# Adaptive modulation weights as 64 rows by two column halves: two transposes per chunk in place of four

## The chip, the cores and the metric

The kernel runs on one core of a Trainium2 chip. Its engines are TensorE (PE, with its weight loads shown as PEld), VectorE (DVE), ScalarE (ACT), GpSimd (POOL) and SyncE (SP), which issues most of the loads and stores. Each engine works through its own queue in order and waits on semaphores for the others. The metric is the device time of one execution in microseconds, the median of several runs. Lower is better.

## The reference

Two decoder layers over 1024 tokens of width 1024, all in float32: first an mLSTM layer, then a layer of multi-head latent attention, each followed by a squared-ReLU MLP. Every norm is modulated by vectors that are computed from one condition vector `c`:

```python
def modulate(h, shift, scale):
    return h * (1 + scale[:, None, :]) + shift[:, None, :]

cond = jax.nn.silu(c)                              # (1, 1024)
for l in range(2):
    ada = cond @ ada_w[l] + ada_b[l]               # (1, 6144) from a 1024 x 6144 matrix
    sh1, sc1, g1, sh2, sc2, g2 = jnp.split(ada, 6, axis=-1)
    h = modulate(rmsnorm(x, norm_g[l, 0]), sh1, sc1)
    ...                                            # mixer: mLSTM (l = 0) or latent attention (l = 1)
    x = x + g1[:, None, :] * rmsnorm(y, norm_g[l, 1])
    h = modulate(rmsnorm(x, norm_g[l, 2]), sh2, sc2)
    y = jnp.square(jax.nn.relu(h @ mlp_w1[l])) @ mlp_w2[l]
    x = x + g2[:, None, :] * rmsnorm(y, norm_g[l, 3])
# before the attention layer, for the shared keys and values:
kv_shift, kv_scale = jnp.split(cond @ kv_ada_w + kv_ada_b, 2, axis=-1)
```

The change touches only `cond @ ada_w + ada_b` and `cond @ kv_ada_w + kv_ada_b`: vector times matrix, one number per column.

## The kernel before

Activations are kept with features on the 128 partitions and 512 tokens (one of two halves of the sequence) along the free dimension. Every large product is done as three matmuls on a high and a low part of each operand (`mm3`, lines 299 to 301). Weights are loaded by SP into one of four buffers `raw` of 128 x 1024 (`fill_raw`, line 266); `wsplit` makes the high part on ScalarE (line 246) and the low part on VectorE (line 247), into a ring of eight buffers `ws`. `split_mod` does the same for activations (lines 520 and 521). Line 255 is a helper under which evacuations and other prompt steps are recorded, line 259 the copy out of PSUM.

The modulation vectors are not computed on TensorE, apart from the first two, but on VectorE beside the other work. A chunk is 512 columns of the matrix, with its 1024 rows as eight blocks of 128. `ada_chunk` loads the chunk in four quarters, each of two row blocks. A quarter goes into a `raw` buffer as one load of 512 KB; while `spare[0]` is set, into an `hd` buffer (a ring of eight, line 403); and while `apart[0]` is set, into two of six `tmc` buffers, as two loads of 256 KB (line 398). Row blocks lie on the partitions, so block `k` is multiplied by `cond[:, k:k+1]`, one number per partition, and added to the accumulator `acc`, the only buffer `tma` (lines 409 and 411): eight VectorE instructions of 512 columns. After two further turns of the generator `ada_turn` transposes the four blocks of 128 columns of `acc` on TensorE into a PSUM buffer `pc` (line 383), VectorE sums over the 512 columns in groups of 128 (line 385), which gives four numbers per partition, and adds the bias (line 386). So each column of the matrix ends on one partition, in the form in which the norms use it.

There are 24 chunks: eight for layer 0 (`bg0`), four for keys and values and four for layer 1 (`bg1`), and eight more for layer 1 (`bg_rest`). They are generators, advanced one step at a time beside the dense work: `with_bg` and the loop over `og0` in the first layer; `behind(bg_latent(), 5)` beside the first MLP, with `apart[0]`; `bg_rest` as the filling of `two_streams` beside the rest of that MLP and the attention of the first half.

The order on TensorE around these places is fixed by `issue_after` edges (`go`, `in_turn`), and the sums are put behind an instruction of the dense stream by `paced`. What else runs on VectorE, ScalarE and SP is put in order, when the program is built, by the framework's own model of how long instructions take, with a priority for `wload` and `evac`. That model also chooses which `raw` buffer a load takes.

Other lines that the prediction names: 889 scales the output of an mLSTM chunk on VectorE, and 915 transposes it on TensorE; 1151 loads stored sums (`s`) for the MLP into `raw`, 1290 and 1291 load weights of the MLP's second matrix; 1666 is another sum over rows, of 128 columns, in the same accumulator `tma`; 1918 is the sum over a row of attention scores, and 2027 transposes the attention's probabilities through `pc`.

Of the kernel before, what the change touches and what calls it, by code (L numbers as in the profile page):

```python
# [9 lines left out]
F32 = mybir.dt.float32  # L10
# [4 lines left out]
ALU = mybir.AluOpType  # L15
AX = mybir.AxisListType

P = 128
# [3 lines left out]
KD = D // P  # L22
# [60 lines left out]
def kernel(  # L83
# [27 lines left out]
    nc = tc.nc  # L111
# [4 lines left out]
    ts = lambda i, n: slice(i * n, (i + 1) * n)  # L116
# [21 lines left out]
    def tmc(dt=F32):  # L138
        return sb.tile([P, 512], dt, tag="tmc", bufs=TMC, name=f"tmc_{next(uid)}")

    def tma():
        return sb.tile([P, 512], F32, tag="tma", bufs=1, name=f"tma_{next(uid)}")

    def small(n, dt=F32):
        return sb.tile([P, n], dt, tag=f"sm{n}", bufs=6, name=f"sm_{next(uid)}")

    def ps():
        return pp.tile([P, 512], F32, tag="ps", bufs=2, name=f"ps_{next(uid)}")

    def pc():  # L150
        return pp.tile([P, 512], F32, tag="pc", bufs=2, name=f"pc_{next(uid)}")
# [7 lines left out]
    def const(shape, dt, name):  # L159
        return sb.tile(shape, dt, tag=name, bufs=1, name=name)  # L160
# [70 lines left out]
    def paced():  # L231

        return tc.issue_after(pace[0]) if pace[0] else nullcontext()
# [59 lines left out]
    def wcols(w, c0, n=P, k0=0, nk=KD):  # L293
        return w[k0 * P : (k0 + nk) * P, c0 : c0 + n].rearrange("(k p) n -> p k n", p=P)
# [37 lines left out]
    cond = const([P, KD], F32, "cond")  # L332
# [44 lines left out]
    ada = const([P, 2, 48], F32, "ada")  # L377
    kvada = const([P, 16], F32, "kvada")

    def ada_turn(acc, bias, dst):  # L380
        pt = pc()
        for j in range(4):
            nc.tensor.transpose(pt[:, ts(j, P)], acc[:, ts(j, P)], ident)
        s = small(4)
        nc.vector.reduce_sum(s, pt.rearrange("p (j k) -> p j k", k=P), axis=AX.X)
        nc.vector.tensor_add(dst, s, bias)
        yield

    late, apart, spare = [False], [False], [False]

    def ada_chunk(w, c0, bias, dst):

        acc = tma()
        for q in range(4):
            if apart[0]:
                r = [tmc(), tmc()]
                for kk in range(2):
                    nc.sync.dma_start(r[kk], w[ts(2 * q + kk, P), c0 : c0 + 512])
            else:
                r = (hdv if spare[0] else raw)()  # L400
                if not spare[0]:
                    r = r.rearrange("p (a b) -> p a b", b=512)
                nc.sync.dma_start(r, wcols(w, c0, 512, 2 * q, 2))
                r = [r[:, 0], r[:, 1]]
            for kk in range(2):
                k = 2 * q + kk
                with paced():
                    if k == 0:
                        nc.vector.tensor_scalar(acc, r[kk], cond[:, 0:1], None, ALU.mult)
                    else:  # L410
                        nc.vector.scalar_tensor_tensor(
                            acc, r[kk], cond[:, k : k + 1], acc, ALU.mult, ALU.add
                        )
            yield
        yield
        late[0] = True
        yield "wait"
        late[0] = False
        yield from ada_turn(acc, bias, dst)

    def ada_part(l, part):
        for j in (2 * part, 2 * part + 1):
            yield from ada_chunk(
                ada_w[l], j * 512, col(AB + l * 48 + j * 4, 4), ada[:, l, ts(j, 4)]
            )

    def ada_kv(part):
        for j in (2 * part, 2 * part + 1):
            yield from ada_chunk(kv_ada_w, j * 512, col(KVB + j * 4, 4), kvada[:, ts(j, 4)])
# [2180 lines left out]
    acc = [m0[:, 0], m0[:, 1], m1[:, 0], m1[:, 1], ps(), ps()]  # L2610
# [64 lines left out]
    def chain(*gs):  # L2675
        for g in gs:
            yield from g() if callable(g) else g
# [65 lines left out]
        drain(wide)  # L2743

    bgs = chain(bg0, bg1)
    with tc.issue_after(loaded):
        for b in range(4):
            nc.sync.dma_start(
                xt_d[0][2 * b * P : (2 * b + 2) * P].rearrange("(k p) n -> p k n", p=P), xT0.t[b]
            )  # L2750
# [375 lines left out]
```

## Time and profile before

| | |
|---|---|
| time, median of 3 runs | 2269.22 us (2268.82 to 2272.16) |
| the profiled execution: time, span | 2272.61 us, 2270.8 us |
| granted TensorE clock, mean | 0.997 of full |
| TensorE busy | 2238.3 us, 99% |
| VectorE busy | 1669.0 us, 73% |
| ScalarE busy | 1113.0 us, 49% |
| moved by DMA | 494.60 MB, mean 218 GB/s |

The span goes from the first to the last instruction of the profiled execution; its time has a little around it. Busy times are unions of an engine's instructions; matmuls are pipelined and overlap in the rows, so the sum of single durations is more than the busy time. In a row of the profile, `L411 DVE SCALAR_TENSOR_TENSOR tma<-raw,cond,tma x103: 732/746/754` means line 411, on VectorE, output and inputs by the program's names without buffer numbers, 103 instructions, and shortest, median and longest duration in ns. `SPq` is SP's queue, where issuing a load is an instruction of its own.

### The profile page before, as it was taken

How to read it: one execution, taken by the hardware profiler on the slowest of the kernel's cores; microseconds unless marked ns; L12 is line 12 of the kernel's file. 1: busy time of each engine (PE TensorE's matmuls, PEld its weight loads, DVE VectorE, ACT ScalarE, POOL GpSimd, SP SyncE). 2: the span in 40 equal slices, each digit the busy share in tenths (PEclk: the TensorE clock that was granted, in tenths of full speed). 3: DMA queues.
4: the chain of work that ended last, by engine and by line, in shares of the span. 5: the costliest groups of instructions: out<-in, count | busy, mean ns of one | idle time of the engine just before them, and what ended most of it. 6: DMA issues, size and time to landing. Idle time of an engine off the chain costs nothing.

```text
span 2270.8 us, 30938 instructions
## 1 busy us (share of the span) xinstructions
PE 2238.3 (99%) x11050; PEld 1852.5 (82%) x11050; DVE 1669.0 (73%) x2717; ACT 1113.0 (49%) x1937; POOL 137.8 (6%) x238
## 2 busy tenths in 40 slices
PE   8999999999999999999999999999999999999998
PEld 6888888888887887778888877888888888888887
DVE  6677777889887787677774787777758967675556
ACT  4455434765434445544455555545545433464343
POOL 1000000001122220000000000000010111100000
PEclk9999999999999999999999999999999999999999
DMA  9544455667999888567687764874487777665431
GB/s 313 186 135 123 148 166 150 194 213 267 323 282 310 280 285 297 178 216 221 208 269 224 262 226 146 285 281 177 156 259 275 240 248 222 234 220 187 149 101 57
DMA packets 404651, 494.60 MB, mean 218 GB/s; under 512 B 29236, under 2 KB 270961, under 8 KB 404497
## 3 DMA queue, kind: packets, MB, share of 16 engines
q1 hardware_dynamic: 384320, 421.74, 57.7%
q0 software_dynamic: 20176, 70.89, 8.6%
q8 instruction: 87, 1.43, 0.3%
q14 instruction: 68, 0.55, 0.1%
HBM read 366.19 MB, written 126.35 MB: 217 GB/s over the span
## 4 chain that ended last, share of the span: by engine, by line
PE 82%; DVE 6%; DMA 5%; issue 4%; ACT 3%; POOL 0%; SPq 0%; DVEq 0%; ACTq 0%; POOLq 0%
PE ps L299 13%; PE ps L300 13%; PE ps L301 13%; PE pm L300 9%; PE pm L301 9%; PE pm L299 9%; DMA raw<-in_mlp_w_dram 2%; PE pc L299 2%; PE pc L301 2%; PE pc L300 2%; DVE wl L247 1%; PE pc L2113 1%; DMA raw<-s 1%; DVE k L255 1%; DMA lw<-wh 1%
## 5 line engine op out<-in xcount | busy, mean ns | idle before, releaser
L246 ACT CAST wh<-raw 128x1024 fp32r<-128x1024 f32 (+4 forms) x295 | 298.6, 1014 | 399.0 <-PE ps L300 140.4
L247 DVE TENSOR_TENSOR wl<-raw,wh 128x1024 fp32r<-128x1024 f32 (+4 forms) x295 | 347.8, 1181 | 173.9 <-ACT wh L246 147.0
L299 PE MATMUL ps<-k,wh 128*128 128x512 f32 x1109 | 438.9, 396 | 2.7 <-DVE k L521 1.2
L301 PE MATMUL ps<-k,wl 128*128 128x512 f32 x1109 | 432.6, 390 | 0.0
L300 PE MATMUL ps<-k,wh 128*128 128x512 f32 x1109 | 432.1, 390 | 0.0
L299 PEld LDWEIGHTS ps<-k,wh 128*128 128x128 f32 x1109 | 208.3, 188 | 50.1 <-issue 3.2
L301 PEld LDWEIGHTS ps<-k,wl 128*128 128x128 f32 x1109 | 208.2, 188 | 44.1
L300 PEld LDWEIGHTS ps<-k,wh 128*128 128x128 f32 x1109 | 208.4, 188 | 42.9 <-issue 1.4
L299 PE MATMUL pm<-wh,hd 128*128 128x512 f32 x488 | 191.6, 393 | 0.0
L301 PE MATMUL pm<-wh,hd 128*128 128x512 f32 x488 | 190.0, 389 | 0.0
L300 PE MATMUL pm<-wl,hd 128*128 128x512 f32 x488 | 189.9, 389 | 0.0
L255 DVE TENSOR_TENSOR k<-k,pm 128x512 f32<-128x512 f32 (+1 forms) x170 | 141.1, 858 | 63.7 <-PE pm L301 63.6
L300 PEld LDWEIGHTS pm<-wl,hd 128*128 128x128 f32 x488 | 91.7, 188 | 19.3 <-issue 0.5
L301 PEld LDWEIGHTS pm<-wh,hd 128*128 128x128 f32 x488 | 91.6, 188 | 19.1
L299 PEld LDWEIGHTS pm<-wh,hd 128*128 128x128 f32 x488 | 91.6, 188 | 19.1 <-issue 0.5
L299 PE MATMUL pm<-hd,wk 128*128 128x512 f32 x256 | 101.5, 396 | 2.0 <-ACT hd L520 2.0
L300 PE MATMUL pm<-hd,wk 128*128 128x512 f32 x256 | 100.2, 391 | 0.4 <-DVE hd L521 0.4
L301 PE MATMUL pm<-hd,wk 128*128 128x512 f32 x256 | 100.0, 391 | 0.0
L300 PE MATMUL pm<-hd,wh 128*128 128x512 f32 x256 | 99.6, 390 | 0.2 <-DVE hd L521 0.2
L299 PE MATMUL pm<-hd,wh 128*128 128x512 f32 x256 | 99.3, 390 | 0.5 <-ACT hd L520 0.5
L301 PE MATMUL pm<-hd,wl 128*128 128x512 f32 x256 | 99.6, 389 | 0.0
L1007 ACT ACTIVATE tmp<-tmp 128x512 f32<-128x512 f32 x80 | 50.4, 630 | 80.1 <-DVE tmp L255 71.0
(510 smaller groups left out, 4750.7 us busy)
## 6 DMA issues: line engine op xcount, KB each, us to landing
raw<-in_mlp_w_dram SPq DMA_DIRECT2D x158, 512.0 KB, 4.9
raw<-in_mlp_w_dram SPq DMA_DIRECT2D x128, 256.0 KB, 4.7
raw<-in_ada_w_dram SPq DMA_DIRECT2D x54, 512.0 KB, 4.7
raw<-in_a_w_in_dram SPq DMA_DIRECT2D x44, 512.0 KB, 4.0
lo<-wl POOLq DMA_DIRECT2D x32, 512.0 KB, 6.1
u<-k POOLq DMA_DIRECT2D x32, 512.0 KB, 5.2
raw<-s SPq DMA_DIRECT2D x32, 512.0 KB, 4.3
wk<-lo SPq DMA_DIRECT2D x64, 256.0 KB, 4.4
```

What stands on the lines that cost most here:

```text
L246: nc.scalar.copy(hi[:, :n], r[:, :n])
L247: i = nc.vector.tensor_sub(lo[:, :n], r[:, :n], hi[:, :n].bitcast(F32))
L255: return f(*a, **k)
L299: nc.tensor.matmul(o, lh, rh, start=start, stop=False)
L300: nc.tensor.matmul(o, lh, rl, start=False, stop=False)
L301: pe_last[0] = nc.tensor.matmul(o, ll, rh, start=False, stop=stop)
L1007: nc.scalar.activation(s, s, AF.Relu)
L2113: nc.tensor.transpose(pt[:, ts(m, P)], u.prs[i][kb // 4][:, ts(kb % 4, P)], ident)
```

## The change

A chunk keeps its 512 columns and 1024 rows but lies otherwise on the partitions: partitions 0 to 63 hold the first 256 columns and partitions 64 to 127 the second 256 columns, of the same 64 rows. So a chunk is 16 row blocks of 64 rows, of 256 columns each. A quarter has four of these blocks and is loaded in two parts, one for each half of the partitions (two buffers `tmc` in four). The multipliers have to lie accordingly: `cond2[64 g + p, 2 k + e]` is `cond[64 e + p, k]` for both halves `g`, made by four small copies. The accumulator has 256 columns, so there are two blocks to transpose; after the transposition the two halves lie beside each other along the free dimension, and the sum goes over groups of 64. The four numbers come in the order (block, half), and the addition of the bias puts them into the order of the columns.

```diff
+    cond2 = const([P, 2 * KD], F32, "cond2")
+
+    def halves_of_cond():
+        v = cond2.rearrange("p (k e) -> p k e", e=2)
+        for g in range(2):
+            for e in range(2):
+                nc.vector.tensor_copy(v[ts(g, 64), :, e], cond[ts(e, 64)])
+
     def ada_turn(acc, bias, dst):
-        pt = pc()
-        for j in range(4):
+        pt = pc()[:, :256]
+        for j in range(2):
             nc.tensor.transpose(pt[:, ts(j, P)], acc[:, ts(j, P)], ident)
         s = small(4)
-        nc.vector.reduce_sum(s, pt.rearrange("p (j k) -> p j k", k=P), axis=AX.X)
-        nc.vector.tensor_add(dst, s, bias)
+        nc.vector.reduce_sum(s, pt.rearrange("p (a k) -> p a k", k=64), axis=AX.X)
+        v = lambda t: t.rearrange("p (g j) -> p j g", j=2)
+        nc.vector.tensor_add(v(dst), s.rearrange("p (j g) -> p j g", g=2), v(bias))
         yield
...
-        acc = tma()
+        acc = tma()[:, :256]
+        by = lambda r: r.rearrange("p (a b) -> p a b", b=256)
         for q in range(4):
             if apart[0]:
-                r = [tmc(), tmc()]
-                for kk in range(2):
-                    nc.sync.dma_start(r[kk], w[ts(2 * q + kk, P), c0 : c0 + 512])
+                r = [by(tmc()), by(tmc())]
             else:
-                r = (hdv if spare[0] else raw)()
-                if not spare[0]:
-                    r = r.rearrange("p (a b) -> p a b", b=512)
-                nc.sync.dma_start(r, wcols(w, c0, 512, 2 * q, 2))
-                r = [r[:, 0], r[:, 1]]
-            for kk in range(2):
-                k = 2 * q + kk
+                r = [by((hd if spare[0] else raw)())]
+            n = 4 // len(r)
+            for i, t in enumerate(r):
+                for g in range(2):
+                    rows, c = 256 * q + 64 * n * i, c0 + 256 * g
+                    nc.sync.dma_start(
+                        t[ts(g, 64)],
+                        w[rows : rows + 64 * n, c : c + 256].rearrange("(k r) n -> r k n", r=64),
+                    )
+            for i in range(4):
+                a, k = r[i // n][:, i % n], 4 * q + i
                 with paced():
                     if k == 0:
-                        nc.vector.tensor_scalar(acc, r[kk], cond[:, 0:1], None, ALU.mult)
+                        nc.vector.tensor_scalar(acc, a, cond2[:, 0:1], None, ALU.mult)
                     else:
                         nc.vector.scalar_tensor_tensor(
-                            acc, r[kk], cond[:, k : k + 1], acc, ALU.mult, ALU.add
+                            acc, a, cond2[:, k : k + 1], acc, ALU.mult, ALU.add
                         )
             yield
...
     bgs = chain(bg0, bg1)
+    halves_of_cond()
```

## The prediction

> **What bounds the kernel now.** I read the page from the top, then the tile that the change touches, then the places where the chain of waits leaves TensorE. First the page's span, its busy times and its chain's shares:
>
> ```profile
> span 2270.8 us, 30938 instructions
> ...
> PE 2238.3 (99%) x11050; PEld 1852.5 (82%) x11050; DVE 1669.0 (73%) x2717; ACT 1113.0 (49%) x1937; POOL 137.8 (6%) x238
> ...
> PE 82%; DVE 6%; DMA 5%; issue 4%; ACT 3%; POOL 0%; SPq 0%; DVEq 0%; ACTq 0%; POOLq 0%
> ```
>
> TensorE is busy for all but 32 us, so TensorE work that disappears is worth its own time, unless something else is then late. The other engines cost time only where the chain passes through them. Next the tile view of `tma`, the accumulator of the modulation sums:
>
> ```profile
> L411 DVE SCALAR_TENSOR_TENSOR tma<-raw,cond,tma x103: 732/746/754, 57.3 to 1243.1; 128x512 f32<-128x512 f32 x103
> ...
> L383 PE MATMUL pc<-ident,tma x96: 270/272/330, 93.8 to 1244.9; 128*128 128x128 f32 x96
> ...
> L1666 DVE SCALAR_TENSOR_TENSOR tma<-tmc,ada,tma x21: 343/352/353, 759.1 to 819.7; 128x128 f32<-128x128 f32 x21
> ...
> L409 DVE TENSOR_SCALAR tma<-raw,cond x15: 475/479/488, 56.8 to 1190.2; 128x512 f32<-128x512 f32 x15
> ...
>   DMA raw<-in_kv_ada_w_dram: 11.2, 4
> ```
>
> The 96 transposes at four a chunk say that there are 24 chunks, between 57 and 1245 us. The last row says that VectorE stood still four times, 11.2 us together, for weights of such a chunk.
>
> **Transposes: 48 go.** A transpose shows as 272 ns, but neighbours overlap; what counts is how far four of them push the next matmul. One of the 24 places, in order of time:
>
> ```profile
> 581.37 0.39 PE L300 MATMUL ps<-k,wh 128*128 128x512 f32 x1
> 581.59 0.39 PE L301 MATMUL ps<-k,wl 128*128 128x512 f32 x1
> 581.82 0.60 PE L383 MATMUL pc<-ident,tma 128*128 128x128 f32 x4
> 582.18 0.47 PE L299 MATMUL ps<-k,wh 128*128 128x512 f32 x1
> 582.49 0.39 PE L300 MATMUL ps<-k,wh 128*128 128x512 f32 x1
> ```
>
> Plain matmuls start 0.225 us apart here. From 581.59 to 582.49 there would be two such steps, 0.45 us, and there are 0.90: the four cost 0.45 us, 0.11 each. 48 x 0.11 = 5.3 us less.
>
> The Trainium skill (TensorE: Matmul & The Clock Gate, Part 4: PE-mode transpose) gives some 275 ns for a transpose within a kernel, as the row's 272 does for one alone. An estimate from that figure would be 48 x 0.275 = 13.2 us less; the starts above show that most of it overlaps, and the sum goes by them.
>
> **Reduction: half as long.** Rows of the groups by form and of the timeline, and the one wait of TensorE for it in the table of waits:
>
> ```profile
> L385 DVE TENSOR_REDUCE sm<-pc 128x4 f32<-128x512 f32 x24 | 16.5, 686 | 7.9 <-PE pc L383 7.8
> ...
> 985.50 0.42 DVE L1918 TENSOR_REDUCE sm<-pm 128x1 f32<-128x256 f32 x1 [0.57 <-ACT raw L1919]
> ...
> PE pc L2027 <- DVE sm L385: 2.7, 2, 2.2
> ```
>
> 0.69 becomes about 0.42. Twice TensorE's transposes at L2027 wait for it, for the PSUM bank it reads: 2 x 0.27 = 0.5 us less. The rest is VectorE's alone.
>
> **Sums: 16 instructions of 256 columns in place of 8 of 512.** No row has this shape. By a line through 128 columns (352 ns) and 512 (746), 256 take 0.48 us; the multiply without a sum, between half of its 479 and the whole, 0.36. Four sums take 1.93 us where two took 1.49: +0.43 for each quarter of a chunk. A chunk costs VectorE 0.36 + 15 x 0.48 + 0.42 = 8.0 us in place of 0.48 + 7 x 0.75 + 0.69 = 6.4: +1.6, and +38 us over 24 chunks. The bounds are 0.37 (half of 746, nothing fixed in an instruction: no change) and 0.55 (midway between 352 and 746: +2.6 a chunk). Four copies of eight columns for `cond2`, each surely below the 0.35 us of 128 columns, are 1.4 us at most, once, beside the first weights; they reach the end only if VectorE has no gap there. What hides the 38 us are VectorE's gaps, by the table of stages:
>
> ```profile
> 322.00:368.00 46.00, 45.64 (x294) 37.53 (x291) 28.37 (x79) 16.27 (x39) 0.56 (x1) 1.00 0.38 110
> 510.90:681.20 170.30, 170.30 (x764) 140.57 (x763) 151.80 (x217) 76.92 (x112) 24.69 (x38) 1.00 0.89 290
> 964.00:1014.00 50.00, 47.79 (x234) 39.21 (x233) 39.51 (x72) 22.19 (x42) 0.00 (x0) 1.00 0.75 243
> ```
>
> (Columns: stage, length, busy PE, weight loads, VectorE, ScalarE, GpSimd, clock, DMA share, GB/s.) The middle stage has seven chunks and VectorE already at 151.8 of 170.3 us; 7 x 1.6 = 11 more still fit, and TensorE has no gap in it, so I take nothing there.
>
> **Loads: two of 64 partitions in place of one of 128.** 69 loads of 512 KB (54 + 10 + 5 in the rows below) become 138 of 256 KB, and 54 of 256 KB (32 + 22) become 108 of 128 KB: 123 more issues on SP's queue. Each takes 0.33 to 0.37 us there, 43 us in all over 1200 us, and everything behind it on SP (the weight loads of L266, L1151, L1290 and the stores) issues that much later.
>
> ```profile
> L403 SPq DMA_DIRECT2D raw<-in_ada_w_dram x54: 367/368/754, 52.7 to 1215.3; - x54
> L403 SPq DMA_DIRECT2D hd<-in_ada_w_dram x10: 367/441/1094, 210.1 to 267.2; - x10
> ...
> L398 SPq DMA_DIRECT2D tmc<-in_ada_w_dram x32: 327/334/3169, 585.1 to 656.7; - x32
> L398 SPq DMA_DIRECT2D tmc<-in_kv_ada_w_dram x22: 327/340/1130, 533.5 to 584.4; - x22
> ...
> raw<-in_kv_ada_w_dram SPq DMA_DIRECT2D x5, 512.0 KB, 4.0
> ...
> raw<-in_a_w_in_dram SPq DMA_DIRECT2D x44, 512.0 KB, 4.0
> ...
> raw<-in_mlp_w_dram SPq DMA_DIRECT2D x158, 512.0 KB, 4.9
> raw<-in_mlp_w_dram SPq DMA_DIRECT2D x128, 256.0 KB, 4.7
> ...
> raw<-in_a_w_in_dram SPq DMA_DIRECT2D x2, 272.0 KB, 2.8
> ```
>
> The rows of the weights shrink from 2 KB to 1 KB. `in_a_w_in` comes mostly in rows of 512 B and lands in the same 4.0 us, so shorter rows cost nothing. When is the pair down? The second half is issued 0.37 us later. If a half alone lands in 2.8 us, as 272 KB did, the pair is there at 3.2, 0.8 earlier than now; if the halves follow one another, at 2 x 2.8 = 5.6, 1.6 later. I take +0.37 (issue alone), between -0.8 and +1.6, since for `in_mlp_w` 256 KB and 512 KB land alike (4.7 and 4.9).
>
> **Where these delays reach the end.** In the chain of waits two stretches run through these sums. The first, while `raw` (four buffers) serves the chunk and the projections in turn:
>
> ```profile
> 330.22 3.63 DMA raw<-in_kv_ada_w_dram
> ...
> 341.36 4.20 DMA raw<-in_kv_ada_w_dram
> 345.59 0.76 DVE tma L411
> 347.04 1.23 DVE wl L247
> 348.29 4.26 DMA raw<-in_kv_ada_w_dram
> ...
> 362.00 0.70 DVE tmc L889
> ...
> PE pc L915 <- DVE tmc L889: 0.4, 1, 0.4
> ```
>
> A split frees a buffer, the load of the sums takes it, VectorE waits in its queue until it has landed, and the mLSTM step behind it (L889, for which TensorE's transposes wait) is late. TensorE lost only 0.4 us at the end of it, so it is just in time there, and the next delay is felt. Three links: each +0.43 for the sums and +0.37 for the load. The second stretch:
>
> ```profile
> 975.31 0.76 DVE tma L411
> 976.09 4.45 DMA raw<-s
> ...
> 982.84 0.74 DVE tma L411
> 983.59 1.13 DVE k L255
> ...
> PE pm L299 <- ACT hd L520: 2.0, 2, 1.5
> ```
>
> Here the sums free the buffer for a weight load (L1151) and stand ahead of the product's evacuation: two more links. TensorE waits 2.0 us in the stage already. Five links x 0.80 = 4.0 us back.
>
> **Sum.** -5.3 - 0.5 + 4.0 = -1.8 us. The profiled execution took 2272.61 us (span 2270.8), the median of the three runs is 2269.22, 3.4 less; the difference is applied to the median: 2267.4 us. In general it is -5.8 + 5 x (0.43 + x), with x the added landing time. The three runs spread over 3.3 us; a change below 0.2%, 4.5 us, I count as none. With x from -0.8 to +1.6 this case alone runs from 2261.6 to 2273.6.
>
> **Rivals.**
> *All hidden.* The links are not tight: VectorE's waits of 11.2 us cost TensorE only 0.4, and finer instructions leave it room. Then -5.8 us, 2263.4. For it: the stages where TensorE has no gap. Against: the chain passes through the sums in two places. It decides when less than 1.3 us of the 4.0 come back.
>
> *The halves follow one another.* Both halves of a pair go through the same queue, and `raw` is held until the second has landed and been summed. At x = 1.6 each link costs 2.0 us, and the SP loads behind them (two at each place: the next projection's weights and the next `raw<-s`) start late by as much once more, 4 x 1.2: -5.8 + 10.1 + 4.8 = +9.1 us, 2278.3. Without the second effect it is +4.3, so it is slower from x = 1.65 alone, or from x near 1.0 with it. For it: the three loads of 3.6 to 4.3 us that stand in the chain, with VectorE idle behind them. Against: the 4.7 and 4.9 us of `in_mlp_w`, by which the time to landing is mostly not the bytes'.
>
> The Trainium skill speaks for this rival: DMA: Bandwidth & Descriptors, Rules for kernel authors, advises against two transfers to disjoint partition halves, since they serialize, and SBUF — State Buffer, Door 1, says that 64 partitions reach only half the ports. No transfer to 64 partitions of this size is in this trace, so no row bears on it; by that rule the time is this rival's 2278.3.
>
> *Another order.* The framework orders VectorE's, ScalarE's and SP's instructions by a model of their durations, and 246 loads in place of 123 and 384 sums in place of 192 give another order, also where nothing is edited. Single stalls in this trace are 1.5 and 2.2 us long (the two waits above); two gained or lost move the time by 4 us either way, 2263.4 or 2271.4, and with the 43 us of SP a few more.
>
> **Chances.** The forecast's case with its small orders, within 0.2%: 0.46. All hidden, faster: 0.25. Halves that follow one another, slower: 0.13. Another order: 0.16, half of it each way. So faster 0.33, same 0.46, slower 0.21. The range takes in the first two whole, nearly all of the order's and the lower part of the halves': 2259 to 2277.
>
> **What would show it.** L383 with 48 transposes; L411 at 0.48 us in 360 instructions; L385 at 0.42; VectorE near 1707 us. Loads of 256 KB to 64 partitions landing in about 4 us, and VectorE's wait for `in_kv_ada_w` still near 11 us. TensorE's busy time 5 us lower and its idle time 4 higher, at 345 to 365 and 975 to 1014 us. The forecast is wrong if TensorE's idle time stays at 32 us (hidden), if those landings are above 5 us (halves), or if the new idle time lies where no modulation chunk is (order).

## The result: 3.8% slower, and the profile after

| | before | after |
|---|---|---|
| median of four runs each, on one chip | 2270.69 us | 2355.94 us (2354.22 to 2358.78) |
| ratio, with its 95% interval | | 1.0376 (1.0358 to 1.0394) |
| span of the profiled execution | 2270.8 us | 2355.4 us |
| granted TensorE clock, mean | 0.997 | 0.987 |
| time in which TensorE worked at half clock, from the trace's clock record | 10.2 us | 45.7 us |

One of the ten executions of g3 below ran at a granted clock of 0.654 and took 3185.77 us; its ratio leaves it out, its median does not.

The prediction was 2267.4 us with a range to 2277; a loss of 85 us came instead. First the page of the kernel after: span, busy times, the granted clock by fortieths, and the chain.

```profile
span 2355.4 us, 31182 instructions
...
PE 2281.5 (97%) x11002; PEld 1858.7 (79%) x11002; DVE 1698.6 (72%) x2913; ACT 1113.0 (47%) x1937; POOL 138.1 (6%) x238
...
PEclk9999989999999999999999999999999999999999
...
PE 82%; DVE 7%; DMA 6%; ACT 2%; issue 1%; SPq 1%; POOL 0%; DVEq 0%; ACTq 0%; POOLq 0%
...
L299 PE MATMUL ps<-k,wh 128*128 128x512 f32 x1109 | 448.4, 404 | 5.7 <-ACT tmp L2075 2.0
L301 PE MATMUL ps<-k,wl 128*128 128x512 f32 x1109 | 441.9, 399 | 0.2 <-DVE wl L247 0.2
L300 PE MATMUL ps<-k,wh 128*128 128x512 f32 x1109 | 441.7, 398 | 0.0
...
L299 PE MATMUL pm<-wh,hd 128*128 128x512 f32 x488 | 191.8, 393 | 0.0
...
raw<-in_ada_w_dram SPq DMA_DIRECT2D x108, 256.0 KB, 5.0
```

TensorE has 48 small instructions fewer and yet is busy 43 us longer (2238.3 before), and it stands still for 74 us instead of 32.5. The half clock explains 18 of the 43 (half of 45.7 - 10.2 us). VectorE's share did not even rise. The rows of the matmuls say more than the totals (in `ps<-k,wh` the first operand, `k`, moves and the second, `wh`, lies as weights). Before, they were:

```profile
L299 PE MATMUL ps<-k,wh 128*128 128x512 f32 x1109 | 438.9, 396 | 2.7 <-DVE k L521 1.2
L301 PE MATMUL ps<-k,wl 128*128 128x512 f32 x1109 | 432.6, 390 | 0.0
...
L299 PE MATMUL pm<-wh,hd 128*128 128x512 f32 x488 | 191.6, 393 | 0.0
```

The matmuls with `k` moving and `wh` or `wl` as weights are slower than before, while those with `wh` moving and `hd` as weights (393 ns) are not.

The table of waits of TensorE, kernel after. Its first row has no counterpart before:

```profile
PE pc L392 <- DVE tma L424: 33.1, 8, 10.5
PE pc L2040 <- DVE sm L394: 4.3, 2, 3.8
PE ps L334 <- POOL ident masks.py:199: 3.1, 1, 3.1
```

Eight times the transposes wait for the last sum of their chunk. The tile view of `tma`, kernel after, with the sums that they wait for:

```profile
L424 DVE SCALAR_TENSOR_TENSOR tma<-raw,cond,tma x221: 460/483/489, 59.3 to 1318.7; 128x256 f32<-128x256 f32 x111
L424 DVE SCALAR_TENSOR_TENSOR tma<-tmc,cond,tma x102: 472/484/906, 570.9 to 719.2; 128x256 f32<-128x256 f32 x102
...
L392 PE MATMUL pc<-ident,tma x48: 270/272/476, 96.9 to 1319.8; 128*128 128x128 f32 x48
```

The longest of the eight, in VectorE's timeline and then in the windows of the same place (length, busy PE, weight loads, DVE, ACT, POOL, granted clock, DMA share, GB/s):

```profile
319.85 0.42 DVE L394 TENSOR_REDUCE sm<-pc 128x4 f32<-128x256 f32 x1 [1.04 <-PE pc L392]
320.19 0.34 DVE L422 TENSOR_SCALAR tma<-raw,cond 128x256 f32<-128x256 f32 x1
...
321.19 5.16 DVE L424 SCALAR_TENSOR_TENSOR tma<-raw,cond,tma 128x256 f32<-128x256 f32 x10
327.52 1.22 DVE L247 TENSOR_TENSOR wl<-raw,wh 128x1024 fp32r<-128x1024 f32 x1 [1.17 <-ACT wh L246]
...
331.22 1.52 DVE L424 SCALAR_TENSOR_TENSOR tma<-raw,cond,tma 128x256 f32<-128x256 f32 x3
```

```profile
319.80:333.00 13.20, 2.72 (x21) 2.02 (x20) 10.87 (x22) 2.42 (x3) 0.00 (x0) 0.67 0.52 150
333.00:347.00 14.00, 14.00 (x65) 11.21 (x66) 10.55 (x31) 4.88 (x10) 0.00 (x0) 0.82 0.78 189
```

Ten sums stand in a row, 5.16 us, 0.52 each although one lasts 0.48. TensorE has 2.72 us of work in 13.2, and runs at less than full clock in this window (0.67) and in the 14 us behind it (0.82). So there are three losses to explain: waits, half clock behind them, and slower matmuls in stretches where nothing waits.

For the slower matmuls I counted, over all neighbouring matmuls of the whole trace, the distance between two starts in whole nanoseconds, in two bins:

```
                        0.222 to 0.231 us   0.232 to 0.239 us
before                          7562             578
after                           4226            3819
```

With the operands' tiles read from the program: of the steps with `k` moving and `wh` or `wl` as weights, 7% are in the slow bin before and 72% after; with `wh`, `wl` or `wk` as one and `hd` as the other operand, 1 to 5% and 5 to 11%. The change itself allocates one thing between `k` and `wh`: `cond2`, 64 bytes a partition. Before, a `k` tile and a `wh` tile lie a multiple of 512 bytes apart. Afterwards everything behind `cond2` is 64 bytes further on.

### The profile page after: what moved, and what is told of

It reads as the page before. It is cut to its first block, busy times and chain, and to the rows that moved or that the text cites. A ratio compares the mean times of both kernels' runs of the same rounds, so it can differ in the third digit from the quotient of the medians.

```text
span 2355.4 us, 31182 instructions
## 1 busy us (share of the span) xinstructions
PE 2281.5 (97%) x11002; PEld 1858.7 (79%) x11002; DVE 1698.6 (72%) x2913; ACT 1113.0 (47%) x1937; POOL 138.1 (6%) x238
## 4 chain that ended last, share of the span: by engine, by line
PE 82%; DVE 7%; DMA 6%; ACT 2%; issue 1%; SPq 1%; POOL 0%; DVEq 0%; ACTq 0%; POOLq 0%
PE ps L299 14%; PE ps L301 13%; PE ps L300 13%; PE pm L300 9%; PE pm L301 9%; PE pm L299 9%; PE pc L299 2%; PE pc L300 2%; PE pc L301 2%; DVE tma L424 1%; DVE wl L247 1%; DMA tmc<-in_ada_w_dram 1%; DMA raw<-in_mlp_w_dram 1%; PE pc L2126 1%; DMA raw<-s 1%
## 5 line engine op out<-in xcount | busy, mean ns | idle before, releaser
L299 PE MATMUL ps<-k,wh 128*128 128x512 f32 x1109 | 448.4, 404 | 5.7 <-ACT tmp L2075 2.0
L301 PE MATMUL ps<-k,wl 128*128 128x512 f32 x1109 | 441.9, 399 | 0.2 <-DVE wl L247 0.2
L300 PE MATMUL ps<-k,wh 128*128 128x512 f32 x1109 | 441.7, 398 | 0.0
L424 DVE SCALAR_TENSOR_TENSOR tma<-raw,cond,tma 128x256 f32<-128x256 f32 x221 | 106.1, 480 | 23.5 <-DMA raw<-in_kv_ada_w_dram 9.2
```

The source lines that it names most:

```text
L299: nc.tensor.matmul(o, lh, rh, start=start, stop=False)
L300: nc.tensor.matmul(o, lh, rl, start=False, stop=False)
L301: pe_last[0] = nc.tensor.matmul(o, ll, rh, start=False, stop=stop)
L424: nc.vector.scalar_tensor_tensor(acc, a, cond2[:, k : k + 1], acc, ALU.mult, ALU.add)
```

## The experiments

Times are medians of several executions; "before" is the kernel before, run beside them on the same chip, and a ratio is to it.

### The sums

**e1**, sums of half the length on the kernel before:

```diff
-                with paced():
-                    ... sum of r[kk] into acc
+                for s in (slice(0, 256), slice(256, 512)):
+                    with paced():
+                        ... sum of r[kk][:, s] into acc[:, s]
```

> The kernel before (loads, four transposes, reduction as they were), with each sum of 512 columns done as two of 256. Theory A (the sums: VectorE needs 1.7 us more a chunk, has no room for it where the chunks follow each other every 11.4 us, and the transposes, whose place on TensorE is fixed, wait for the last sum): most of the loss returns, 2330 to 2370 us, TensorE waiting some 25 to 45 us for the sums at its transposes, and the half-clock stretches come with these waits. Theory B (the loads: 123 more issues on SP and pairs of 64 partitions): 2270 to 2280 us, no such waits.

2273.20 us, ratio 1.0015 (1.0005 to 1.0024). Twice the number of sums costs 3.6 us. That looked like an acquittal of the sums, and it was a wrong test: the two halves are two independent chains, which the changed kernel does not have.

**e5**, the changed kernel with half of its sums:

```diff
-            for i in range(4):
+            for i in range(0, 4, 2):
```

> The changed kernel with every second sum left out (half of the rows are not added; loads and transposes as changed). Theory A: the waits at the transposes go, and the 5.3 us of the 48 transposes show: 2258 to 2270 us. Theory B (loads): the waits stay, 2320 us or more.

2322.32 us, 1.0232 (1.0216 to 1.0247): 34 us of the 85 go with half of the sums. By its time this is Theory B, but the waits did not stay, as B has it: those of the transposes fall from 33.1 to 12.2 us. So the sums matter, and are not all.

**e4**, the changed kernel, transposes of the chunks beside the dense stage one turn later:

```diff
+        if apart[0]:
+            yield "wait"
```

> The changed kernel, with the transposes of a chunk one half step of the dense stream later, only beside the first MLP (the seven chunks whose weights go into tmc). Theory A with fixed places for the transposes: their waits there (20 us in seven, and some 10 us of half clock behind them) go, 2320 to 2335 us; the waits elsewhere (332, 1044, 1255 us) stay. Theory B (loads late): the sums end no earlier and the wait only shrinks by the half step, 2335 to 2350 us. If VectorE is short over the whole stretch, not only between two chunks, the time is given back at its end and stays near 2350.

2362.10 us, 1.0407 (1.0392 to 1.0423). The transposes' waits halve to 16.3 us, and L1701, the transposes of the next task (L1699 in the changed kernel), now waits 16.1 us for its sums, where the changed kernel has no such row: the chunks end later, so what follows them does too. A wait at a fixed place of the order cannot be pushed away while the work in front of it is too long.

**e7**, the kernel before, sums of half the length that all depend on one another (the edit is shown against e1):

```diff
                 for s in (slice(0, 256), slice(256, 512)):
+                    o = acc[:, :256]
                     with paced():
-                        ... r[kk][:, s] into acc[:, s]
+                        ... r[kk][:, s] into o
...
-            nc.tensor.transpose(pt[:, ts(j, P)], acc[:, ts(j, P)], ident)
+            nc.tensor.transpose(pt[:, ts(j, P)], acc[:, ts(j % 2, P)], ident)
```

> The kernel before with every sum of 512 columns as two of 256, all 16 of a chunk into the same accumulator of 256 columns, so that each reads what the one ahead of it wrote. It mixes the two column halves (the sums of both go into one accumulator, transposed twice), so its output is not the reference's; loads, transposes and addresses are as before. If dependence alone costs what the two chains gave back: 2270 + 27 = 2297. If it costs 2 us at each of the five chunks whose sums end under 1 us ahead of their transposes, and some half-clock time behind these: 2280 to 2288. If it needs the late loads: 2274.

2317.35 us, 1.0207 (1.0192 to 1.0222): 47 us, more than any of my cases, with whole loads, four transposes and unmoved tiles. It differs from e1 in the dependence (and in one multiply a chunk that became a sum). Its waits and one chunk of its VectorE:

```profile
PE pc L383 <- DVE tma L415: 31.6, 7, 10.4
```

```profile
626.23 1.00 DVE L415 SCALAR_TENSOR_TENSOR tma<-tmc,cond,tma 128x256 f32<-128x256 f32 x2
627.14 0.68 DVE L526 TENSOR_TENSOR hd<-tmp,hd 128x512 fp32r<-128x512 f32 x1
627.75 1.52 DVE L415 SCALAR_TENSOR_TENSOR tma<-tmc,cond,tma 128x256 f32<-128x256 f32 x3
...
632.17 2.56 DVE L415 SCALAR_TENSOR_TENSOR tma<-tmc,cond,tma 128x256 f32<-128x256 f32 x5
```

Five dependent sums take 2.56 us. In e1, three independent ones:

```profile
601.29 1.27 DVE L414 SCALAR_TENSOR_TENSOR tma<-tmc,cond,tma 128x256 f32<-128x256 f32 x3
```

Over all neighbouring sums, the median step is 0.52 us in e7 and in the changed kernel, 0.40 in e1, and 0.79 for the 512 columns before. A sum that reads what the one ahead of it wrote starts 0.036 us after that one's end; one that does not starts 0.08 us before it. So 16 sums take 8.3 us dependent and 6.3 independent, and 8 long ones 6.3: the same. In e7's profiled execution TensorE stands still 67.7 us, 35 more than before, nearly all of it in the 31.6 of this row, and is busy 2247.6 us, 9 more; 27.2 us of work at half clock in place of 10.2 account for 8.5 of these. So its 44.5 us of longer span are the waits and the half clock behind them.

Much of this is order. Between the transposes of the seventh and the eighth chunk TensorE has 69 other matmuls before and in e1, 21 in e7 and 19 in the changed kernel: the framework's order puts the transposes ahead of work that used to cover the sums, and that is the wait of over 10 us. On VectorE, other work stands between the last eight sums of the tenth chunk (8 instructions of 8.2 us in e7, one of 0.7 in e1) and of the sixteenth (10 of 7.4 us, against 3 of 2.0). In e7 the tenth chunk ends so:

```profile
570.13 0.48 DVE L415 SCALAR_TENSOR_TENSOR tma<-tmc,cond,tma 128x256 f32<-128x256 f32 x1
570.53 1.22 DVE L247 TENSOR_TENSOR wl<-raw,wh 128x1024 fp32r<-128x1024 f32 x1
571.66 1.22 DVE L255 TENSOR_TENSOR k<-k,pm 128x1024 f32<-128x1024 f32 x1
572.79 0.48 DVE L415 SCALAR_TENSOR_TENSOR tma<-tmc,cond,tma 128x256 f32<-128x256 f32 x1
...
576.59 0.48 DVE L415 SCALAR_TENSOR_TENSOR tma<-tmc,cond,tma 128x256 f32<-128x256 f32 x1
...
577.59 0.48 DVE L415 SCALAR_TENSOR_TENSOR tma<-tmc,cond,tma 128x256 f32<-128x256 f32 x1
```

At these three places the transposes wait 10.4, 6.4 and 4.6 us in e7 and 10.5, 6.3 and 4.3 in the changed kernel, about two thirds of the 31.6 and 33.1 us. In the three chunks in a row with 48 matmuls between their transposes, in all of these kernels, they wait 2.2 to 2.7 us in e7 because the sums no longer fit. The other order stands in e7 and in the changed kernel, where each sum needs the one ahead of it, and not in e1; so e7's 47 us are the dependence together with the order that the build gives to it. No run holds the order and changes the step alone.

### The loads

**e2**, the kernel before with half loads:

```diff
-                    nc.sync.dma_start(r[kk], w[ts(2 * q + kk, P), c0 : c0 + 512])
+                    for g in range(2):
+                        nc.sync.dma_start(r[kk][ts(g, 64)], w[ts(4 * q + 2 * kk + g, 64), c0 : c0 + 512])
...
-                nc.sync.dma_start(r, wcols(w, c0, 512, 2 * q, 2))
+                for g in range(2):
+                    nc.sync.dma_start(r[ts(g, 64)], wcols(w, c0, 512, 2 * q, 2)[ts(g, 64)])
```

> The kernel before (sums of 512 columns, four transposes), with each load of modulation weights split into two of 64 partitions, rows still 2 KB long. Theory A (the sums): 2268 to 2280 us, TensorE waits under 5 us for the sums. Theory B (the loads): 2330 to 2370 us, with the waits at the transposes as in the changed kernel.

2294.09 us, 1.0102 (1.0085 to 1.0119): 24 us for the loads alone.

**g3**, the same number of loads, each over all 128 partitions:

```diff
+                    for g in range(2):
+                        nc.sync.dma_start(r[kk][:, ts(g, 256)], w[ts(2 * q + kk, P), c0 + 256 * g : c0 + 256 * g + 256])
...
+                for g in range(2):
+                    nc.sync.dma_start(r[:, :, ts(g, 256)], wcols(w, c0 + 256 * g, 256, 2 * q, 2))
```

> The kernel before with every load split by columns, two of 256 columns over all 128 partitions (rows of 1 KB); as many loads as with the half loads of 64 partitions, which took 24 us. Theory N (the number of loads costs: each is one more issue of some 0.35 us on SP ahead of the others): 2294. Rival H (a load of 64 partitions is what is slow): 2270. If short rows cost as well: over 2300.

2274.21 us, 1.0020 (1.0010 to 1.0030): 4 to 5 us, near the rival's 2270 and far from 2294. Rows of 1 KB and 123 more issues are nearly harmless; 64 partitions are not. SP's issues and the landings, e2 first and then g3:

```profile
L407 SPq DMA_DIRECT2D raw<-in_ada_w_dram x108: 595/604/1493, 51.4 to 1241.0; - x108
```

```profile
raw<-in_ada_w_dram SPq DMA_DIRECT2D x108, 256.0 KB, 5.3
```

```profile
L408 SPq DMA_DIRECT2D raw<-in_ada_w_dram x108: 367/446/1515, 51.6 to 1219.5; - x108
```

```profile
raw<-in_ada_w_dram SPq DMA_DIRECT2D x108, 256.0 KB, 4.3
```

Over 64 partitions 256 KB take 0.60 us of SP and land in 5.3; over 128, 0.45 and 4.3. Where the trace tells both landings of a pair (43 of e2's 54, 42 of the changed kernel's, 41 of g3's), the second half is down 6.7 us after the first issue in e2, 6.1 in the changed kernel and 5.0 in g3 (medians), against 4.7 for the whole load.

**h2** and **h3**, e2's edit in one branch only, the chunks loaded apart (beside the dense stage) and the others:

```diff
 h2: e2's first hunk alone
 h3: e2's second hunk alone
```

> The kernel before with half loads of 64 partitions only in the chunks that load their tiles apart (tmc, from 425 us on, beside the dense matmuls); the others as before. In the kernel with all loads halved the transposes waited 10.2 us there, and the half-clock time grew from 16.6 to 30.2 us. Theory P (the cost is where the sums end less than 1 us ahead of the transposes): about 2290, nearly all of the 24 us. Rival Q (a cost spread over all loads): some 10, since 64 of 123 loads' pairs are here: 2280.

> The counterpart: half loads only in the chunks that load into raw and hd, those loaded apart as before. Theory P: 2272 to 2275. Rival Q: about 2283.

2281.67 us, 1.0039 (1.0021 to 1.0057), and 2279.58, 1.0035 (1.0024 to 1.0047). The 11 and 9 us are a cost spread over both, nearer to rival Q than to Theory P, and not one of the tight chunks alone. In h2 the transposes wait 5.4 us; h3 has no such row, its loss is in many small ones.

**h1**, whole-width loads in the changed layout, on the kernel with two chains (below):

```diff
-                for g in range(2):
-                    ... t[ts(g, 64)] <- 64 * n rows, 256 columns
+                for m in range(n):
+                    rows = 256 * q + 64 * (n * i + m)
+                    nc.sync.dma_start(t[:, m], w[rows : rows + 64, c0 : c0 + 512].rearrange("r (g n) -> g r n", g=2))
```

> The kernel with the moved tile and two chains, with the same layout of the weights (64 rows by 2 column halves), but each load covers all 128 partitions: one for 64 rows of both halves (rows of 1 KB, 128 KB), four for a quarter of a chunk where there were two of 64 partitions (two instead of two in the chunks that load their tiles apart). Theory H (a load of 64 partitions is what is slow, some 20 of the 24 us of the half loads): 2307 - 20, and some 5 more for more issues, about 2292. Rival N (issues on SP, or the 1 KB rows): 2307 to 2317.

3115.70 us, 1.3704 (1.3681 to 1.3727). Neither theory had this:

```profile
L414 SPq DMA_DIRECT2D raw<-in_ada_w_dram x216: 497/2788/3729, 51.5 to 2057.7; - x108
```

```profile
L373 SPq DMA_DIRECT2D k<-in_x_dram x8: 328/403/2761, 141.8 to 151.5; - x8
```

These loads, whose 128 rows are the two column halves of 64 rows, hold SP for 2.8 us in the median, but not each by itself: of a row of them the first two are issued in 0.53 and 0.50 us (from 170.07 us on) and those behind them in 2.1 to 3.3. A plain load of x behind such a row takes 2.76 us, the others of its line 0.33 to 0.43. So what holds SP is what was issued ahead; why these loads are slow, no run shows. h1 cannot tell H from N.

**f3**, e1's and e2's edits together:

```diff
 e1's loop over two column slices
 e2's two loops over partition halves
```

> The kernel before with both e1's edit (every sum of 512 columns as two of 256) and e2's (every load as two of 64 partitions with rows of 2 KB); four transposes, addresses as before. If the two costs add, 2270 + 4 + 24 = 2298. If they meet at the same transposes (sums that run back to back cannot catch up on a late load), more: the changed kernel's other 86 - 21 us, about 2335, with waits of the transposes for the last sum of some 30 us.

2295.17 us, 1.0116 (1.0101 to 1.0131): the two costs add, and nothing like 2335 comes. What the changed kernel has beyond this is the dependence, the moved tiles and, in its half loads, rows of 1 KB.

### The moved tiles

**f1**, one unused tile on the kernel before, of 64 and of 32 bytes:

```diff
+    const([P, 16], F32, "pad")      # f1_shift_64; [P, 8] in f1_shift_32
```

> The kernel before with one more constant tile of 64 bytes a partition, which nothing writes or reads, at the place where the change has cond2. Everything allocated behind it (wh, wl, hd, tmc and others) lies 64 bytes further on, the k tiles and raw stay; no instruction differs. Theory M (a matmul's moving and stationary operands that lie 64 bytes apart modulo 128 step slower: in the changed kernel 72% of the steps with k moving and wh or wl as weights are 0.2333 us, before 7%): 21 us slower, about 2291, with the share of 0.2333 us steps as in the changed kernel. Rival R (the slower step comes with the change's own instructions or loads): 2270, steps as before.

> The same with a tile of 32 bytes, so that the two operands lie 32 bytes apart modulo 128, a distance that neither kernel has for these matmuls. Theory M says that it differs from 2270 by the steps alone, between no change and the 21 us of 64 bytes; if any distance but none is slow, about 2291; if this distance is better than none, under 2265. Rival R: 2270.

2293.81 us, 1.0106 (1.0091 to 1.0121), and 2293.32, 1.0105 (1.0090 to 1.0120): 25 us for a tile that nothing touches, from the matmuls alone. In the kernel with 64 bytes, in the groups by form:

```profile
L299 PE MATMUL ps<-k,wh 128*128 128x512 f32 x1109 | 444.2, 401 | 1.4 <-DVE k L522 1.0 <-ACT tmp L553 0.2
L301 PE MATMUL ps<-k,wl 128*128 128x512 f32 x1109 | 438.2, 395 | 0.0
L300 PE MATMUL ps<-k,wh 128*128 128x512 f32 x1109 | 437.9, 395 | 0.0
L299 PE MATMUL pm<-wh,hd 128*128 128x512 f32 x488 | 191.8, 393 | 0.0
```

396, 390 and 390 ns became 401, 395 and 395; `hd` with `wh`, which moved together, stays at 393. The slow bin has 3914 steps at 64 bytes and 4157 at 32 (578 before).

**f2** and **g4**, the changed kernel realigned in two ways:

```diff
 f2:
-    cond2 = const([P, 2 * KD], F32, "cond2")
+    cond2 = const([P, 4 * KD], F32, "cond2")[:, : 2 * KD]
 g4: the same line as in the changed kernel, moved up
     dve = nc.vector.memset(ones[:, 0:1], 1.0).ins.engine
+    cond2 = const([P, 2 * KD], F32, "cond2")
```

> The changed kernel with cond2 made 128 bytes a partition (its second half unused), so that the operands behind it lie as before modulo 128; no instruction differs from the changed kernel's otherwise. Theory M: the 0.2333 us steps go back to some 500 of 8,100 and the time falls by 21 us to about 2335, what is left being loads, sums and the waits of the transposes. Rival R: 2356.

> The changed kernel with cond2 allocated right behind the constant ones, so that k, raw, wh, wl and hd all move by the same 64 bytes and lie to each other exactly as in the kernel before; no instruction differs from the changed kernel's. In the realigned try (cond2 of 128 bytes) 51% of the steps with k moving and wh as weights were still slow. Theory M, amended (the two operands must lie at the same place modulo 256 or more, not 128): slow steps back to some 500, and 2353 - 24 = 2332 or a little less. Rival R (the slow step belongs to the changed kernel's own instructions): 2356.

f2: 2352.98 us, 1.0364 (1.0346 to 1.0381), a miss: 128 bytes do not put the old steps back, and 2676 are still in the slow bin. g4: 2334.02 us, 1.0274 (1.0258 to 1.0289), as expected, with 611 steps there (578 before) and its transposes' waits unchanged:

```profile
PE pc L391 <- DVE tma L423: 32.3, 8, 10.4
```

So 22 us of the changed kernel are the place of one tile, and independent of the waits.

### Undoing the dependence, and the gain by itself

**g5**, g4 with two accumulators by turns, and **g6**, g5 without the addition that joins them:

```diff
+        two = tma()
+                s = two[:, ts(k % 2, 256)]
-                        ... sum into acc
+                        ... sum into s
+            if q == 3:                                             # not in g6
+                with paced():                                      # not in g6
+                    nc.vector.tensor_add(acc, acc, two[:, 256:])   # not in g6
```

> The same as the kernel with the moved tile, and the sums go by turns into two accumulators of 256 columns, which one addition joins at the end of a chunk (24 additions more). Theory D (a sum that reads what the sum just ahead of it wrote starts 0.036 us after that one's end, one that does not starts 0.08 us before it: 0.52 us a step against 0.40, so 16 x 0.52 = 8.3 us a chunk against 8 x 0.78 = 6.3 before): the step is 0.40, a chunk's sums take 6.9 us, the transposes' wait for the last sum falls from 33 us to about the 10 of the half loads alone, and the time to about 2300. Rival L (the transposes wait because the loads land late): the wait stays at 33 us and the time within 5 us of the kernel with the moved tile.

> The kernel with the moved tile and two chains without the addition that joins them at the end of each chunk; it leaves out the odd row blocks of the sums. 24 additions of 256 columns stand between the last sum and the transposes. If they carry the 12 us: 2295. If the rows of 1 KB or the other layout carry them: 2303 or more.

g5: 2306.94 us, 1.0165 (1.0143 to 1.0186). The step is 0.40 us, the waits are as many in us as with the half loads alone, and 27 us are back:

```profile
PE pc L391 <- DVE tma L430: 10.5, 6, 2.5
```

The order went back as well: the eighth chunk has 77 other matmuls ahead of its transposes (19 in g4), and between the last sums of the tenth and the sixteenth chunk VectorE has 0.7 and 2.0 us of other work (8.2 and 6.7 in g4). So the 27 us, like e7's 47, are the step and the order together.

g6: 2308.64 us, 1.0163 (1.0146 to 1.0180): the joining addition costs nothing.

**e3**, the kernel before with two of its four transposes:

```diff
-        pt = pc()
-        for j in range(4):
+        pt = pc()[:, :256]
+        for j in range(2):
...
-        ... pt.rearrange("p (j k) -> p j k", k=P)
+        ... pt.rearrange("p (j k) -> p j k", k=64)
```

> The kernel before with two of the four transposes of each chunk, and the reduction over their 256 columns in groups of 64; loads and sums as before. It leaves out half of the columns of the modulation, so its output is not the reference's. It prices the change's gain alone: 48 transposes fewer by 0.11 us and a reduction of 0.42 us in place of 0.69 at the two waits of L2027: 2264. Rival (the transposes lie in gaps that something else sets, or other work moves): 2270.

2267.22 us, 0.9985 (0.9975 to 0.9995): 3.6 us less. That is all that the new layout can earn.

**e6**, another way to be rid of the reduction, on the kernel before:

```diff
-            nc.tensor.transpose(pt[:, ts(j, P)], acc[:, ts(j, P)], ident)
-        s = small(4)
-        nc.vector.reduce_sum(s, pt.rearrange("p (j k) -> p j k", k=P), axis=AX.X)
-        nc.vector.tensor_add(dst, s, bias)
+            nc.tensor.matmul(pt[:, j : j + 1], acc[:, ts(j, P)], ones[:, 0:1], start=True, stop=True)
+        nc.vector.tensor_add(dst, pt[:, :4], bias)
```

> The kernel before with the four transposes and the reduction over 128 columns of each chunk replaced by four matmuls with the chunk's sums as weights and a column of ones moving, which leave the 4 columns in PSUM; the bias is added from there. It takes 0.69 us of VectorE and one link (transposes, reduction, addition) off each of 24 chunks, among them the two waits of 2.6 us for the reduction; TensorE's small matmuls are as many as the transposes. If the end of these chains sets anything: 2264 to 2267. If not: 2270.

2284.45 us, 1.0058 (1.0043 to 1.0074): slower by 15, a miss; its TensorE is busy 2250.0 us, 12 more than before, and each of the 96 new matmuls stands in the trace twice (11146 records instead of 11050). Why, no run shows. No experiment pointed to a version that computes the same and is faster than the kernel before.

### What adds up

Put on the kernel before one at a time: dependent sums, with the order that comes with them, +47, half loads +24, moved tiles +25, transposes -3.6; together 93, against 85 measured. Taken from the changed kernel one after another: moved tiles 22, dependence and order 27, and 37 remain, of which half loads explain 24. The sums' price may be lower in the second way because a transpose waits for the later of load and sum, so that with the loads late quicker sums help less; that is argued, not shown. 12 us between g5 (2307) and f3 (2295) stay open, or 15 with the 3.6 that g5's two transposes should save. g6 rules out the joining addition. TensorE stands still 14 us longer in g5's trace than in f3's, of which 3.8 are in the transposes' row; the 1 KB rows together with half loads, or the order, were not tried.

## Why the prediction was wrong, step by step

**The bound** was read rightly: TensorE sets the time, and each loss showed as TensorE waiting, at half clock, or stepping more slowly.

**Transposes and reduction**, -5.8 us: 3.6 in e3, so the sign was right and the size somewhat large. The reduction does last 0.42 us (L394).

**Sums.** The durations were right (0.48 and 0.34 us); the cost was not, at two steps. First, a duration is not a step. The 0.48 of one sum is 0.40 or 0.52 of the engine's time by whether the next one needs its result, and 1.49 us for two of 512 hid the same 0.08 and 0.036. The rows to see it in were there: the timeline before has sums of 0.75 us with other work between, starting before the previous end. Second, and worst: "7 x 1.6 = 11 more still fit, and TensorE has no gap in it, so I take nothing there". Where I put nothing, five chunks' transposes then waited 16.6 us, and three outside the stage the rest of the 33.1. What I had taken is a mean over a stage of 170 us. The chunks in it are not alike: three have only 48 matmuls between their transposes. Here is one of them before, VectorE and then TensorE:

```profile
602.59 1.21 DVE L255 TENSOR_TENSOR k<-k,pm 128x1024 f32<-128x1024 f32 x1
603.72 0.74 DVE L411 SCALAR_TENSOR_TENSOR tma<-tmc,cond,tma 128x512 f32<-128x512 f32 x1
604.38 1.22 DVE L247 TENSOR_TENSOR wl<-raw,wh 128x1024 fp32r<-128x1024 f32 x1
```

```profile
604.29 0.39 PE L301 MATMUL ps<-k,wl 128*128 128x512 f32 x1
604.61 0.63 PE L383 MATMUL pc<-ident,tma 128*128 128x128 f32 x4
```

The last sum ends at 604.46 and the transposes start at 604.61: a margin of 0.15 us, where 2 us were to be added. Even that is no slack: in the kernel after, where the transposes of the eighth chunk did wait, they start 0.15 us behind their last sum too. Three more chunks beside the dense stage had 0.55 to 0.85. The table of waits before shows nothing there, because a wait that is just avoided has no row. The difference between the last producer and its consumer, chunk by chunk, would have shown it.

**Loads.** 123 more issues is right; 0.33 to 0.37 us each is not, they take 0.60. The added landing x, taken as 0.37, is 1.5 us in the changed kernel (6.1 against 4.7), inside the stated bounds, and 2.0 in e2, above them. But its price was formed with five links, and even at x = 1.5 the prediction's sum gives only -5.8 + 5 x (0.43 + 1.5) = +3.9 us. In e2 the delays act elsewhere and grow: at three transposes beside the dense stage TensorE waits 2.1, 2.6 and 5.5 us for the sums. h2 and h3 show that the cost is spread over both kinds of chunks. Reading only the links that the chain of waits names was the fault: it names those that ended last before, not those that come next.

**The rival with the halves** had the sign and the mechanism and priced them at 9 us above before, against 24 alone. The Trainium skill's rule (DMA: Bandwidth & Descriptors, Rules for kernel authors) not to split a transfer by partition halves was good advice: this trace agrees, 6.7 us for e2's pair against 4.7 for the whole load. That the halves run one after the other is not shown: e2's second half lands 1.1 us behind its first, though issued 0.65 behind it, so it is held up a little, but the rows do not say by what.

**Another order** was put at 4 us either way, by single stalls of 1.5 and 2.2 us. It came, and is much of the loss: at three places with another order the transposes wait 21.1 of the 33.1 us. The largest, the eighth chunk's transposes moved ahead of some 50 matmuls, is a wait of 10.5 us and 5.1 of the 45.7 us of work at half clock.

**`cond2`** was priced by its four copies. Its 64 bytes of place were in no step and cost 22 us. Nothing in the trace of before shows the danger; only that all these matmuls had the same step.

**Half clock** was in no step either: 35 us more of work at half clock cost 18, on top of the waits ahead of it.

**The signs named beforehand** were mostly of durations, and these came nearly as said: sums of 0.48 us, a reduction of 0.42, VectorE busy 1698.6 us (1707 was named), its wait for the weights of keys and values 10.7 us (11). The landings were 4.1 us for these weights and 5.0 for the others, at the bound that was named. Only TensorE's idle time told plainly that the forecast was wrong: 74 us, and it lies at the transposes of the chunks, a place that none of the signs named.

## What to carry to other kernels

Price a chain of dependent instructions by the distance between starts, not by durations; and before work is called hidden, measure for each repetition how long before its consumer the last producer ends, since a mean over the stage hides the full ones. When a change adds a tile, keep the old distances between the operands of the dense matmuls (allocate it ahead of all of them), or every comparison measures that too. An experiment that halves an operation must keep its dependences: e1 acquitted the sums, e7 with the same count and one accumulator convicted them. And where the framework orders the instructions, compare the orders of two kernels before a difference in time is put down to the changed instructions: here the dependence came with another order.

## What the runs showed of the hardware

- Of the distances tried between moving operand and weights, the one before (a multiple of 512 bytes) gave a median matmul step of 0.227 us with `k` and `wh`; with 32, 64 and 128 bytes more, 81, 73 and 48% of these steps took 0.232 us or more, before 7%. Why, no run shows.
- Two of these sums overlap by 0.08 us on VectorE unless the second needs the first's result; then 0.036 us lie between. The Trainium skill (VectorE: DVE Perf Modes, The DRAIN you can't avoid) reports that eight copies took as long with a semaphore behind each as with one behind the last. No run here has that pair: nearly all sums wait for a semaphore of VectorE in both forms (350 of 360 in e7, 317 of 336 in e1), and the dependent form is the slower by 0.12 us a sum.
- TensorE's half-clock stretches last 3.41 us or a multiple of it, apart from the one that the trace's end cuts. In the kernel after, an idle time of 10.48 us that began at 322.4 was followed by 13.65 us from 324.3 on, 5.1 of them with work; one of 2.00 us that began at 628.2 by 3.41 from 631.5, all with work. Before, one of 1.25 us was followed by 3.41, and one of 2.20 by none. The Trainium skill (TensorE: Matmul & The Clock Gate, Part 1) has free-running windows of that length; the lengths agree, and this trace adds that an idle time well below one window can be enough.
- SP's time for one issue (shortest, median) is 0.37 and 0.37 us for 512 KB over 128 partitions, 0.37 and 0.45 for 256 KB over 128, and 0.60 and 0.60 for 256 KB over 64. It also goes by what was issued ahead: behind h1's loads of 128 KB a plain load took 2.76.
